# The root chain of the first attention stage, issued at the seventh matmul of the query product instead of ahead of it

## The chip, the cores and the metric

The kernel runs on one core of a Trainium2 chip. The metric is the device time of one execution in microseconds (us), the median of three runs. A profiled execution gives a trace of the five engines: PE (TensorE; its weight loads are listed apart as PEld), DVE (VectorE), ACT (ScalarE), POOL (GpSimd) and SP, which only issues DMAs here.

## What is computed

One layer of an encoder, for two sequences of 2048 tokens with 1024 features, all in float32. Two kinds of attention share one input projection:

```
h = rms_norm(x, norm_w)
q_a, k_a, v_a, g_a, q_b, k_b, v_b, g_b = split(h @ w_in)
q_a, k_a = rope(rms_norm(q_a)), rope(rms_norm(k_a))      # 8 query heads, 2 key heads of 64
o_a = window_attention(q_a, k_a, v_a, sink) * silu(g_a)   # +-128 tokens
o_b = neighbourhood_attention(q_b, k_b, v_b, rpb) * silu(g_b)
x = x + concat(o_a, o_b) @ w_out
y = x + (p @ w_ple) * sigmoid(x @ w_ple_gate)
```

The change lies in the first stage alone: branch a, the windowed attention.

## The kernel before

The kernel has three stages: windowed attention (token tiles f = 0 to 31, 16 of 128 tokens for each sequence), neighbourhood attention, and the output products. Each float32 operand of a product is split into a rounded part and a remainder, so that each product becomes three matmuls per block of 128 rows; splits are shared out between ACT (the rounded part) and VectorE or POOL (the remainder).

In the first stage, each token tile f passes `proj_a(f)` (L391), a generator with three products: `pk` (keys and values, 24 matmuls of 256 columns), `pq` (queries, 24 of 512) and `pg` (gate, 24 of 512). Attention of a tile is done by `unit_a(f, kv)` (L540), twice for each tile, once for each key head. Its steps are: `sc` (four heads of scores, each two matmuls and, in `softmax`, L214, one VectorE instruction that adds the mask and takes the row maximum, L217), then `exps` (L224: the negated maximum `nm`, L230; four exponentials on ACT, L232; the sink, L236 and L237; and after "den" the denominator L239, its reciprocal L240, a factor L241, and a gate product on POOL, L243), `pt` (three groups of four transposes of the weights, each split by L566 on ACT and L567 on VectorE), `po` (products with the values) and `fin` (two transposes `pgt` of the gate, then the output from L586 on ACT, two L589 and L590 on VectorE).

A list written out by hand, `PLAN_A` (L77), says at which share of a tile's projection cost each step of attention is issued. Projection matmuls of tile f + 2 fill TensorE between the steps of tile f. So in what this document calls a block, one token tile's worth of the stage, TensorE works first through `pq`, then `pg`, then `pk` of the next tile; the first half holds the unit of key head 0, the second that of key head 1. In the first half the four `sc` steps come after 2, 4, 4 and 5 matmuls of `pq`, the step "rest" (the second part of the split of the queries, `split_q`, L248: a copy on ACT, L252, a subtraction on VectorE, L254, a copy on POOL, L256) after 4 and 5, "den" after 11, "fin" after 14, and `pt` from 23.

TensorE's order is fixed by the source (`pinned`). On the other engines an instruction that isn't pinned takes the place in its engine's queue that a planner gives it when the kernel is built: among the instructions that it takes to be ready, the first in the source, so that others fill the gaps of a chain whose steps wait for each other. `P` (L155) pins an instruction behind whatever stands before it in the source on its engine. Each engine then works strictly in the order of its queue.

Around the change, on VectorE: when the last matmul of `pk` has been issued, `proj_a` emits the mean square (L398, L400, pinned), the sums of squares of the two key heads (L403), and then the **root chain**: L407 and L409 (the values under the roots), `rsqrt` (L123: two integer instructions L126 and L128, then three Newton rounds of L131, L132 and L133, on 128x3 values), the halving L411, the scaling of the keys L413, and the rotation `rope` (four POOL instructions, L426 to L429). The chain's results are used by `values` (L417, issued at the 16th matmul of `pq`, PV = 15), by the transposition of the keys in `keys_a` (L379, at the tenth matmul of `pg`) and by the tanh of the gate (L468). At the third and fifth matmul of `pq` the next token tile is split (`split`, L286: a pinned ACT cast L294, a POOL subtraction L295, and a load). At the tenth (PD = 9) `late` issues the gate of the tile before (L471, pinned).

PSUM is shared out by tags. `sc`, `pgt` and `pt` share three slots in turn: in each half, the third group of `pt` gets the slot that `pgt` had, and must wait until L590 has read `pgt`.

Of the kernel before, what the change touches and what calls it, by code (L numbers as in the profile page):

```python
# [11 lines left out]
F32 = mybir.dt.float32  # L12
# [3 lines left out]
ALU = mybir.AluOpType  # L16
# [6 lines left out]
HD = 64  # L23
NEG = -1.0e30
EPS = 1e-6
# [40 lines left out]
PG = (3, 6)  # L66
PV = 15
PD = 9
PB = (26, 30)
TAIL = 9300  # L70
HOLD = {"wa": 20, "wb": 12, "wp": 0}
# [18 lines left out]
def emit(ctx, tc, io):  # L90
    nc = tc.nc
# [31 lines left out]
    def rsqrt(pool, v, y, n, tag):  # L123
        i2 = pool.tile([128, n], I32, tag=tag + "i", name=tag + "i")
        a = pool.tile([128, n], F32, tag=tag + "a", name=tag + "a")
        nc.vector.tensor_scalar(out=i2, in0=v.bitcast(I32), scalar1=1, scalar2=None,  # L126
                                op0=ALU.logical_shift_right)
        nc.vector.tensor_scalar(out=y.bitcast(I32), in0=i2, scalar1=-1, scalar2=0x5F3759DF,  # L128
                                op0=ALU.mult, op1=ALU.add)
        for _ in range(3):  # L130
            nc.vector.scalar_tensor_tensor(out=a, in0=y, scalar=-0.5, in1=y, op0=ALU.mult, op1=ALU.mult)  # L131
            nc.vector.tensor_tensor(out=a, in0=a, in1=v, op=ALU.mult)  # L132
            nc.vector.scalar_tensor_tensor(out=y, in0=a, scalar=1.5, in1=y, op0=ALU.add, op1=ALU.mult)  # L133
# [21 lines left out]
    P = tc.keep_in_program_order  # L155
# [105 lines left out]
    ap = ab_stack.enter_context(tc.tile_pool(name="ab", bufs=1))  # L261
# [37 lines left out]
    def square(f, i):  # L299

        if f >= 2 * NT:
            return
        if i == 0:
            stats[f] = (ap.tile([128, 12], F32, tag="ssq", name="ssq", bufs=3),
                        ap.tile([128, 1], F32, tag="ee", name="ee", bufs=3))
        ssq, ee = stats[f]
        xn = staged.pop(("n", f, i))
        sqr = nc.scalar.activation(xn, xn, AF.Square, accum_out=ssq[:, 10 + i:11 + i])
        if f > 1:
            tc.keep_in_program_order(sqr)  # L310
            load_next()
        if i == 1:
            for dst, src in copies[:CP] if f >= 2 else ():
                tc.keep_in_program_order(nc.sync.dma_start(dst, src))
                copies.pop(0)
# [41 lines left out]
    for i in range(4):  # L357
        nc.vector.tensor_tensor(out=tab[i // 2][:, i % 2], in0=cs[:, i % 2],
                                in1=rw[:, i].unsqueeze(1).broadcast_to([128, NT, 16]), op=ALU.mult)
# [16 lines left out]
    last = {2 * NT - 2: 48, 4 * NT - 2: 24, 6 * NT - 2: 24}  # L376
    HX = {PB[0]: 0, PB[1]: 1}

# [12 lines left out]
    def proj_a(f):  # L391
        s, t = divmod(f, NT)
        xr, ms, (ssq, ee) = xt.pop(f), ms_a[:, f:f + 1], stats.pop(f)
        ka = 22 if f in last else KA
        early = 1 < f < 2 * NT - 1
        pk = ptile([128, 256], "pj", "pk")
        yield from project(pk, xr, lambda k, b: wx[:, k, b, :], 112)
        P(nc.vector.tensor_scalar(out=ms, in0=ssq[:, 10:11], scalar1=ssq[:, 11:12], scalar2=1.0 / DM,  # L398
                                  op0=ALU.add, op1=ALU.mult))
        P(nc.vector.tensor_scalar(out=ee, in0=ms, scalar1=EPS, scalar2=EPS * EPS, op0=ALU.mult, op1=ALU.add))  # L400
        sq2 = ap.tile([128, 512], F32, tag="sq", name="sq2", bufs=2)
        nc.scalar.activation(sq2[:, :128], pk[:, 0:128], AF.Square)
        nc.vector.tensor_reduce(out=ssq[:, 8:10], in_=sq2[:, :128].rearrange("p (h d) -> p h d", d=HD),  # L403
                                op=ALU.add, axis=AX.X)
        vr = ap.tile([128, 11], F32, tag="vr", name="vr", bufs=2)
        y = ap.tile([128, 12], F32, tag="y", name="y", bufs=4)
        nc.vector.tensor_scalar(out=vr[:, 8:10], in0=ssq[:, 8:10], scalar1=1.0 / HD, scalar2=ee,  # L407
                                op0=ALU.mult, op1=ALU.add)
        nc.vector.tensor_scalar(out=vr[:, 10:11], in0=ms, scalar1=EPS, scalar2=None, op0=ALU.add)  # L409
        rsqrt(ap, vr[:, 8:11], y[:, 8:11], 3, "rqk")  # L410
        nc.vector.tensor_scalar_mul(y[:, 11:12], y[:, 10:11], 0.5)  # L411
        kt = ap.tile([128, 4, HD], F32, tag="kt", name="kt", bufs=2)
        nc.vector.tensor_tensor(out=kt[:, 0:2, :], in0=pk[:, 0:128].rearrange("p (h d) -> p h d", d=HD),  # L413
                                in1=y[:, 8:10].unsqueeze(2).broadcast_to([128, 2, HD]), op=ALU.mult)
        pv = pk[:, 128:256].rearrange("p (h d) -> p h d", d=HD)

        def values():  # L417
            P(nc.scalar.activation(vv[:, t, :, 0, :], pv, AF.Copy, scale=y[:, 10:11]))
            P(nc.vector.scalar_tensor_tensor(out=vv[:, t, :, 1, :], in0=pv, scalar=y[:, 10:11],
                                             in1=vv[:, t, :, 0, :].bitcast(F32), op0=ALU.mult, op1=ALU.subtract))  # L420

        def rope(v, n, tb):
            r = ap.tile([128, 2, 8, 16], F32, tag="vr_", name="r", bufs=2)
            cb_ = tab[tb][:, 0, t, :].unsqueeze(1).broadcast_to([128, n, 16])
            sb_ = tab[tb][:, 1, t, :].unsqueeze(1).broadcast_to([128, n, 16])
            nc.gpsimd.tensor_tensor(out=r[:, 0, :n], in0=v[:, :, 0:16], in1=cb_, op=ALU.mult)  # L426
            nc.gpsimd.tensor_tensor(out=r[:, 1, :n, 0:8], in0=v[:, :, 8:16], in1=sb_[:, :, 0:8], op=ALU.mult)
            nc.gpsimd.tensor_tensor(out=r[:, 1, :n, 8:16], in0=v[:, :, 0:8], in1=sb_[:, :, 8:16], op=ALU.mult)
            nc.gpsimd.tensor_tensor(out=v[:, :, 0:16], in0=r[:, 0, :n], in1=r[:, 1, :n], op=ALU.add)  # L429
        rope(kt[:, 0:2, :], 2, 1)  # L430
        yield 0, False
        pq = ptile([128, 512], "pj", "pq")
        for i, c in enumerate(project(pq, xr, lambda k, b: w_q[k][:, b, :], 215)):
            if i in HS and early:
                split(f + 1, HS[i], P)
            if i - 4 in HN and f in last:
                square(f + 1, HN[i - 4])
            if i == PV:
                values()
            if i == PD and late:  # L440
                late.pop()()
            if i == PD + 1 and f == NT + 9:
                stats_b(0)
            yield c
            if i == ka:
                keys_a(kt, t)
        sq = ap.tile([128, 512], F32, tag="sq", name="sq", bufs=2)
        nc.scalar.activation(sq, pq, AF.Square)
        nc.vector.tensor_reduce(out=ssq[:, 0:8], in_=sq.rearrange("p (h d) -> p h d", d=HD), op=ALU.add, axis=AX.X)
        nc.vector.tensor_scalar(out=vr[:, 0:8], in0=ssq[:, 0:8], scalar1=1.0 / HD, scalar2=ee,  # L450
                                op0=ALU.mult, op1=ALU.add)
        rsqrt(ap, vr[:, 0:8], y[:, 0:8], 8, "rqa")
        q = ap.tile([128, 8, HD], F32, tag="qg", name="q", bufs=6)
        nc.vector.tensor_tensor(out=q, in0=pq.rearrange("p (h d) -> p h d", d=HD),  # L454
                                in1=y[:, 0:8].unsqueeze(2).broadcast_to([128, 8, HD]), op=ALU.mult)
        rope(q, 8, 0)
        yield 0, False
        pg = ptile([128, 512], "pj", "pg")
        for i, c in enumerate(project(pg, xr, lambda k, b: w_g[k][:, b, :], 215)):
            if i in HG and f > 0 and not early:  # L460
                split(f + 1, HG[i])
            if i in HN and f > 0 and f not in last:
                square(f + 1, HN[i])
            yield c
            if i + 24 == ka:
                keys_a(kt, t)
        gs = ap.tile([128, 512], F32, tag="qg", name="gs", bufs=6)
        nc.scalar.activation(gs, pg, AF.Tanh, scale=y[:, 11:12])  # L468

        def gate():  # L470
            P(nc.vector.scalar_tensor_tensor(out=gs, in0=gs, scalar=1.0, in1=pg, op0=ALU.add, op1=ALU.mult))  # L471
        if 0 < f < 2 * NT - 2:
            late.append(gate)
        else:
            gate()
        held[f] = q, gs, y
        if t == NT - 1:
            regroup(s)
        else:
            regroup_next()  # L480
        yield 0, False
# [129 lines left out]
    def proj_b(f):  # L611
# [10 lines left out]
        for i, c in enumerate(project(pk, xr, lambda k, b: ready("wa", k, w_qk)[:, b, :], 215)):  # L622
            at = i + 24 if f in last else i
            if i == PD and f == 2 * NT + 9:
                stats_b(1)
# [299 lines left out]
    with tc.tile_pool(name="c", bufs=1) as op:  # L925
# [192 lines left out]
        for m in range(7 * len(groups)):  # L1118
            n, i = divmod(m, 7)
# [104 lines left out]
```

## Time and profile before

| what | value |
|---|---|
| median of 3 runs | 2607.18 us (2605.81 to 2609.73) |
| profiled execution, its own time | 2603.58 us |
| its span, first to last instruction | 2601.7 us |
| TensorE busy in the span | 2547.1 us (98%) |
| VectorE busy | 1963.3 us (75%) |
| ScalarE busy | 1416.3 us (54%) |
| POOL busy | 789.2 us (30%) |
| granted TensorE clock, mean | 0.994 |

How to read the rows that follow: in a timeline or a chain of waits, the first number is the start in us from the span's start, the second the duration in us; then come the engine, the line of the kernel, the operation, the tiles (written <- read), the shapes, and after an x how many instructions the row holds. In brackets behind it stands the time that the engine was idle before, and what ended it. Rows of a wait list give the waiting engine, tile and line, then the one waited for, and the total in us, the number of times, and the longest wait.

### The profile page before, as it was taken

The page shows a single profiled execution, that of the slowest core. Times are in us where ns is not written, and L with a number is a line of the kernel's source. Part 1 is how long each engine was busy: PE and PEld are TensorE (multiplying, and loading weights), DVE is VectorE, ACT ScalarE, POOL GpSimd, SP SyncE. Part 2 cuts the span into 40 slices and gives each one's busy share as a digit, 9 for nine tenths or more (in the row PEclk, how much of TensorE's full clock was granted, in tenths as well). Part 3 has the DMA queues.
Part 4 walks back from the last instruction along what each step waited for, and adds up shares of the span by engine and source line. Part 5 has one row for each costly group of instructions (what it writes and reads, how often), then busy time and mean ns, then how long its engine had stood idle before and what let it go on. Part 6 is the DMA issues. An engine that isn't in the chain of part 4 may idle for free.

```text
span 2601.7 us, 47013 instructions
## 1 busy us (share of the span) xinstructions
PE 2547.1 (98%) x16080; PEld 2269.7 (87%) x16080; DVE 1963.3 (75%) x5702; ACT 1416.3 (54%) x3327; POOL 789.2 (30%) x996
## 2 busy tenths in 40 slices
PE   7999999999999999999999999999989999999999
PEld 6888888888877888888788888887989999999999
DVE  6888988889897788888888888888655648555454
ACT  5666666666675666666766666666432214222222
POOL 3333333333322333333233332321122423233321
PEclk9999999999999999999999999999999999999999
DMA  5333322111143564555654554457575445232221
GB/s 178 108 102 108 101 93 94 54 60 56 58 111 120 174 188 153 185 184 163 225 178 150 187 177 150 153 155 214 172 251 190 150 165 196 82 116 92 78 82 45
DMA packets 227519, 357.51 MB, mean 137 GB/s; under 512 B 37936, under 2 KB 115376, under 8 KB 222128
## 3 DMA queue, kind: packets, MB, share of 16 engines
q1 hardware_dynamic: 227280, 354.50, 42.8%
q8 instruction: 128, 2.10, 0.3%
q14 instruction: 111, 0.91, 0.1%
HBM read 266.33 MB, written 105.92 MB: 143 GB/s over the span
## 4 chain that ended last, share of the span: by engine, by line
PE 87%; DVE 5%; DMA 2%; ACT 2%; issue 2%; POOL 1%; SPq 0%; POOLq 0%; DVEq 0%; ACTq 0%
PE pqk L202 13%; PE pvg L202 12%; PE acca L1034 11%; PE accc L1034 9%; PE pg L202 6%; PE pq L202 5%; PE pob L202 4%; PE pple L202 3%; PE ptb L205 3%; PE scb L202 3%; PE pt L205 3%; PE po L202 3%; PE sc L202 3%; PE pk L202 3%; PE pout L202 3%
## 5 line engine op out<-in xcount | busy, mean ns | idle before, releaser
L232 ACT ACTIVATE s<-s,nm 128x384 f32<-128x384 f32 (+4 forms) x512 | 306.2, 599 | 340.6 <-DVE nm L228 185.0
L202 PE MATMUL pvg<-wb,xr 128*128 128x512 f32 x1536 | 455.2, 404 | 0.0
L202 PE MATMUL pqk<-wa,xr 128*128 128x512 f32 x1536 | 437.4, 407 | 0.0
L295 POOL TENSOR_TENSOR xr<-stx,xr 128x512 fp32r<-128x512 f32 x192 | 247.6, 1297 | 193.4 <-ACT xr L294 189.9
L202 PEld LDWEIGHTS pqk<-wa,xr 128*128 128x128 f32 x1536 | 267.5, 189 | 37.2
L202 PEld LDWEIGHTS pvg<-wb,xr 128*128 128x128 f32 x1536 | 267.4, 189 | 31.3
L202 PE MATMUL pg<-wb,xr 128*128 128x512 f32 x768 | 232.4, 410 | 4.1 <-DVE q L454 4.1
L202 PE MATMUL pq<-wa,xr 128*128 128x512 f32 x768 | 222.8, 404 | 3.6 <-ACT wa L147 2.8
L243 POOL TENSOR_TENSOR g<-qg,rd 128x256 f32<-128x256 f32 x64 | 39.7, 620 | 495.1 <-DVE rd L241 481.3
L1034 PE MATMUL acca<-opd,s 128*128 128x256 f32 x1344 | 164.6, 283 | 2.9 <-ACT r L1066 2.5
L1034 PEld LDWEIGHTS acca<-opd,s 128*128 128x128 f32 x1344 | 162.7, 192 | 3.6 <-ACT r L1066 2.7
L202 PEld LDWEIGHTS pq<-wa,xr 128*128 128x128 f32 x768 | 141.1, 191 | 28.3 <-ACT wa L147 3.4
L217 DVE CUSTOM_DVE_ANT_0 s<-scb,bias 128x288 f32<-128x288 f32 (+3 forms) x256 | 142.0, 555 | 29.1 <-PE scb L202 23.6
L202 PEld LDWEIGHTS pg<-wb,xr 128*128 128x128 f32 x768 | 137.9, 190 | 25.0 <-issue 4.6
L726 ACT CAST p_t<-ptb 96x384 fp32r<-96x384 f32 (+3 forms) x256 | 129.7, 508 | 54.1 <-PE ptb L205 52.3
L727 DVE TENSOR_TENSOR p_t<-ptb,p_t 96x384 fp32r<-96x384 f32 (+3 forms) x256 | 149.0, 584 | 9.1 <-ACT p_t L726 6.4
L607 ACT ACTIVATE ks_b<-pktb,wk 64x128 fp32r<-64x128 f32 x256 | 125.4, 490 | 49.1 <-DVE ks_b L608 40.6
L202 PEld LDWEIGHTS pob<-p_t,vw 128*128 128x128 f32 (+2 forms) x832 | 133.2, 190 | 20.8 <-DVE p_t L727 2.5
L608 DVE SCALAR_TENSOR_TENSOR ks_b<-pktb,wk,ks_b 64x128 fp32r<-64x128 f32 x256 | 115.1, 449 | 39.8 <-ACT ks_b L607 33.4
L202 PE MATMUL pob<-p_t,vw 128*128 128x256 f32 (+2 forms) x832 | 141.0, 283 | 2.0 <-DVE p_t L727 2.0
L1000 POOL TENSOR_TENSOR opd<-sum,opd 128x1024 fp32r<-128x1024 f32 x28 | 69.5, 2484 | 232.6 <-ACT opd L986 232.6
L217 DVE CUSTOM_DVE_ANT_0 s<-sc,mask 128x384 f32<-128x384 f32 (+1 forms) x256 | 135.8, 532 | 0.8
(197 smaller groups left out, 5909.1 us busy)
## 6 DMA issues: line engine op xcount, KB each, us to landing
stx<-x_b SPq DMA_DIRECT2D x128, 256.0 KB
vw<-v_d SPq DMA_DIRECT2D x112, 256.0 KB
stx<-x_a SPq DMA_DIRECT2D x64, 256.0 KB
stn<-x_n SPq DMA_DIRECT2D x64, 256.0 KB
v_d<-vb SPq DMA_DIRECT2D x64, 256.0 KB
x1r<-x_d SPq DMA_DIRECT2D x16, 1024.0 KB
y_t<-r SPq DMA_DIRECT2D x64, 256.0 KB
v_d<-vb SPq DMA_DIRECT2D x96, 128.0 KB
```

What stands on the lines that cost most here:

```text
L202: pinned(nc.tensor.matmul(out, lhsT, rhs, start=start, stop=stop))
L205: pinned(nc.tensor.transpose(out, in_, ident))
L217: nc.vector.tensor_tensor_reduce(out=s[:, :n], in0=ps[:, :n], in1=bias, scale=1.0, scalar=-3.0e38, op0=ALU.add, op1=ALU.max, accum_out=sm[ ...
L232: nc.scalar.activation(ss[i][:, :n], ss[i][:, :n], AF.Exp, bias=nm[:, i:i + 1], accum_out=den[:, i:i + 1])
L243: nc.gpsimd.tensor_tensor(out=g2, in0=gs.rearrange("p (h d) -> p h d", h=4), in1=rd.unsqueeze(2).broadcast_to([128, 4, HD]), op=ALU.mult)
L295: nc.gpsimd.tensor_tensor(out=lo, in0=raw, in1=hi.bitcast(F32), op=ALU.subtract)
L607: nc.scalar.activation(hi, pkt[a:a + 64, i], AF.Copy, scale=wk[a:a + 64, 1:2])
L608: nc.vector.scalar_tensor_tensor(out=lo, in0=pkt[a:a + 64, i], scalar=wk[a:a + 64, 1:2], in1=hi.bitcast(F32), op0=ALU.mult, op1=ALU.subtract)
L726: nc.scalar.copy(p_t[:kc, :nch, 0], pf)
L727: nc.vector.tensor_tensor(out=p_t[:kc, :nch, 1], in0=pf, in1=p_t[:kc, :nch, 0].bitcast(F32), op=ALU.subtract)
L1000: each(lambda x, y, z: eng.tensor_tensor(out=x, in0=y, in1=z, op=ALU.subtract), out, a, b)
L1034: pinned(nc.tensor.matmul(ps[:, kk], w[k][:, a, c:c + 128], o[:, b, k], start=i in (0, 1, 4) and kk == 0 and k == 0 and j == 0, stop=k == ...
```

## The change

The root chain, the scaling of the keys and their rotation become a function `roots`. For the first two token tiles it is called where the code stood; for all others at the seventh matmul of `pq` (PC = 6), which in the source is behind the four `sc` steps, `nm`, and the VectorE instruction of "rest" (L254). Its first instruction is pinned.

```diff
+PC = 6
...
-        nc.vector.tensor_scalar(out=vr[:, 8:10], in0=ssq[:, 8:10], scalar1=1.0 / HD, scalar2=ee,
-                                op0=ALU.mult, op1=ALU.add)
-        nc.vector.tensor_scalar(out=vr[:, 10:11], in0=ms, scalar1=EPS, scalar2=None, op0=ALU.add)
-        rsqrt(ap, vr[:, 8:11], y[:, 8:11], 3, "rqk")
-        nc.vector.tensor_scalar_mul(y[:, 11:12], y[:, 10:11], 0.5)
-        kt = ap.tile([128, 4, HD], F32, tag="kt", name="kt", bufs=2)
-        nc.vector.tensor_tensor(out=kt[:, 0:2, :], in0=pk[:, 0:128].rearrange("p (h d) -> p h d", d=HD),
-                                in1=y[:, 8:10].unsqueeze(2).broadcast_to([128, 2, HD]), op=ALU.mult)
...
-        rope(kt[:, 0:2, :], 2, 1)
+        kt = ap.tile([128, 4, HD], F32, tag="kt", name="kt", bufs=2)
+
+        def roots():
+
+            P(nc.vector.tensor_scalar(out=vr[:, 8:10], in0=ssq[:, 8:10], scalar1=1.0 / HD, scalar2=ee,
+                                      op0=ALU.mult, op1=ALU.add))
+            nc.vector.tensor_scalar(out=vr[:, 10:11], in0=ms, scalar1=EPS, scalar2=None, op0=ALU.add)
+            rsqrt(ap, vr[:, 8:11], y[:, 8:11], 3, "rqk")
+            nc.vector.tensor_scalar_mul(y[:, 11:12], y[:, 10:11], 0.5)
+            nc.vector.tensor_tensor(out=kt[:, 0:2, :], in0=pk[:, 0:128].rearrange("p (h d) -> p h d", d=HD),
+                                    in1=y[:, 8:10].unsqueeze(2).broadcast_to([128, 2, HD]), op=ALU.mult)
+            rope(kt[:, 0:2, :], 2, 1)
+        if f < 2:
+            roots()
         yield 0, False
         pq = ptile([128, 512], "pj", "pq")
         for i, c in enumerate(project(pq, xr, lambda k, b: w_q[k][:, b, :], 215)):
...
+            if i == PC and f > 1:
+                roots()
             if i == PV:
                 values()
```

## The prediction

> **What bounds the kernel now.** I read the page first, then the chain of waits over one block of the first attention stage, then the wait list of that stage, then the timeline of each engine in that block.
>
> ```profile
> PE 87%; DVE 5%; DMA 2%; ACT 2%; issue 2%; POOL 1%; SPq 0%; POOLq 0%; DVEq 0%; ACTq 0%
> ```
>
> TensorE is 87% of the chain that ended last. So an edit that moves only vector work counts only where it changes a wait of TensorE. The chain of one steady block (it starts with the query product at 309.95; start us, us, what) shows where such a wait is:
>
> ```profile
> 318.91 0.44 PE pt L205 x4
> ...
> 320.04 0.66 PE pt L205 x4
> ```
>
> Two groups of four transposes of the same size, 0.44 and 0.66 us: the third group (pt2) pays 0.66 - 0.44 = 0.22 us. The weight loads of TensorE in the timeline of the block, and the wait list from 60 to 770 us (us in total, times, longest), name the cause:
>
> ```profile
> 320.04 0.42 PEld L205 LDWEIGHTS pt<-ident,s 128*128 128x128 f32 x4 [0.44 <-DVE ot L590]
> ```
>
> ```profile
> PEld pt L205 <- DVE ot L590: 12.1, 26, 1.3
> ```
>
> pt2 needs the PSUM slot of pgt, and L590 is the last reader of pgt. It happens 26 times, nearly once in each block. **So the change is worth what it does to the end of L590 in the first half of a block**, 26 times over: 26 x 0.22 = 5.7 us if the wait goes altogether, and one for one in the other direction, since TensorE already waits there. VectorE in that half (start us, duration, instruction):
>
> ```profile
> 310.99 0.55 DVE L217 CUSTOM_DVE_ANT_0 s<-sc,mask 128x384 f32<-128x384 f32 x1
> ...
> 313.29 0.98 DVE L128 TENSOR_SCALAR y<-rqki 128x3 int32<-128x3 int32 x1
> 314.19 0.54 DVE L217 CUSTOM_DVE_ANT_0 s<-sc,mask 128x384 f32<-128x384 f32 x1
> ...
> 314.77 0.16 DVE L230 SCALAR_TENSOR_TENSOR nm<-mx,snk 128x4 f32<-128x4 f32 x1
> ...
> 315.05 0.15 DVE L133 SCALAR_TENSOR_TENSOR y<-rqka,y 128x3 f32<-128x3 f32 x1
> 315.24 0.69 DVE L254 TENSOR_TENSOR q<-pqt,q 64x512 fp32r<-64x512 f32 x1
> 315.96 0.16 DVE L131 SCALAR_TENSOR_TENSOR rqka<-y 128x3 f32<-128x3 f32 x1
> 316.16 0.69 DVE L471 SCALAR_TENSOR_TENSOR gs<-gs,pg 128x512 f32<-128x512 f32 x1
> 316.76 0.15 DVE L132 TENSOR_TENSOR rqka<-rqka,vr 128x3 f32<-128x3 f32 x1
> 316.95 0.16 DVE L133 SCALAR_TENSOR_TENSOR y<-rqka,y 128x3 f32<-128x3 f32 x1
> ...
> 317.74 0.15 DVE L411 TENSOR_SCALAR y<-y 128x1 f32<-128x1 f32 x1
> 317.81 0.28 DVE L413 TENSOR_TENSOR kt<-pk,y 128x128 f32<-128x128 f32 x1
> 318.00 0.15 DVE L239 TENSOR_TENSOR den<-den,es 128x4 f32<-128x4 f32 x1
> 318.26 0.18 DVE L240 RECIPROCAL rd<-den 128x4 f32<-128x4 f32 x1
> 318.47 0.23 DVE L241 TENSOR_SCALAR rd<-rd,y 128x4 f32<-128x4 f32 x1
> 318.61 0.85 DVE L589 TENSOR_TENSOR ot<-po,ot 64x256 f32<-64x256 f32 x2
> 319.56 0.42 DVE L590 TENSOR_TENSOR ot<-pgt,ot 128x256 f32<-128x256 f32 x1
> ```
>
> The root chain and the maxima alternate, so the last maximum starts at 314.19 only. The gate of the previous block (L471) falls into the chain too. L590 ends at 319.56 + 0.42 = 319.98.
>
> **The change, part by part.** Thirteen small VectorE instructions before the product (two sums, two integer steps, nine Newton steps), the halving L411, the product L413 and four POOL instructions of the rotation go to the seventh matmul. Nothing is added or taken away, and no DMA is issued by what moves. In the source it passes two splits of the next token tile (ACT casts, POOL subtractions, loads on SP), the maxima, nm, es, and L254. The first moved instruction is pinned behind the VectorE instruction ahead of it in the source, which is now L254. The gate L471 is pinned too, and what stands ahead of it is now L413 instead of L254. So the order becomes: four maxima, nm, es, L254, chain, L413, L471, and the denominator and L589, L590 where they fit.
>
> The maxima. The last score matmul and POOL's second subtraction:
>
> ```profile
> 311.98 0.51 PE L202 MATMUL sc<-ks_a,q 128*128 128x384 f32 x2
> ```
>
> ```profile
> 312.96 1.29 POOL L295 TENSOR_TENSOR xr<-stx,xr 128x512 fp32r<-128x512 f32 x1
> ```
>
> The last maximum can start at 311.98 + 0.51 = 312.49 and, as the fourth of 0.55 from 310.99, ends by 313.2, where it now ends at 314.73. But the next instruction is nm, which reads two tiles in SBUF, and POOL runs from 312.96 to 314.25. What nm does then is seen once, in the last block of the stage, where no chain stands between the maxima and nm (VectorE, then POOL):
>
> ```profile
> 753.60 1.22 DVE L230 SCALAR_TENSOR_TENSOR nm<-mx,snk 128x4 f32<-128x4 f32 x1
> 754.86 0.16 DVE L236 TENSOR_TENSOR es<-snk,nm 128x4 f32<-128x4 f32 x1
> ```
>
> ```profile
> 753.52 2.71 POOL L295 TENSOR_TENSOR xr<-stx,xr 128x512 fp32r<-128x512 f32 x2 [6.63 <-ACT xr L294]
> ```
>
> It took 1.22 us for 0.16. L128 above does the same: its 0.98 ends at 314.27, 0.02 behind POOL. So the hold that L128 pays today is paid by nm instead: nm ends at 314.27, where it now ends at 314.93, a gain of 0.66 and not 1.5. Behind nm on VectorE stand es, L254 and the whole chain; on ACT the four exponentials wait for it.
>
> The Trainium skill has this rule, and it speaks against the change: "SBUF — State Buffer", section "Who interferes with whom", says that a VectorE instruction with two SBUF inputs contends with a GpSimd instruction that reads SBUF, and that one with a single SBUF input outside the two-port modes does not. The trace agrees on both: nm took 1.22, the maxima 0.55. Without the rule the sum would be that of the first rival below.
>
> Then es at 314.27 + 0.04 (754.82 to 754.86) = 314.31, and L254 after it as after L133 now (315.20 to 315.24): 314.31 + 0.16 + 0.04 = 314.51. L254 holds its successor for 315.96 - 315.24 = 0.72: L407 at 315.23. It takes 0.23 like L241, its successor starts 0.04 later: L126 at 315.50. Now the chain runs almost alone, each step waiting for the one ahead: 316.95 to 317.74 is four steps, 0.197 each. From L126 to L411 are eleven steps, 2.17: L411 at 317.67, L413 (0.07 later, as now) at 317.74, L471 (0.19 later) at 317.93, its successor (0.60, as 316.16 to 316.76) at **318.53**. The keys are thus not late (L413 at 317.74, now 317.81). What is late next is what the gate now stands in front of: the denominator and the halves L589.
>
> How far those go into gaps of the chain is not shown for this order. A neighbouring block with shorter rows shows how they can:
>
> ```profile
> 413.30 0.15 DVE L239 TENSOR_TENSOR den<-den,es 128x4 f32<-128x4 f32 x1
> 413.42 0.15 DVE L411 TENSOR_SCALAR y<-y 128x1 f32<-128x1 f32 x1
> 413.49 0.28 DVE L413 TENSOR_TENSOR kt<-pk,y 128x128 f32<-128x128 f32 x1
> 413.69 0.17 DVE L240 RECIPROCAL rd<-den 128x4 f32<-128x4 f32 x1
> 413.77 0.39 DVE L589 TENSOR_TENSOR ot<-po,ot 64x256 f32<-64x256 f32 x1
> 414.08 0.22 DVE L241 TENSOR_SCALAR rd<-rd,y 128x4 f32<-128x4 f32 x1
> 414.34 0.43 DVE L589 TENSOR_TENSOR ot<-po,ot 64x256 f32<-64x256 f32 x1
> 414.87 0.42 DVE L590 TENSOR_TENSOR ot<-pgt,ot 128x256 f32<-128x256 f32 x1
> ```
>
> Here den goes in front of L411, and from L240 to the end of L590 it is 415.29 - 413.69 = 1.60. That is the value I take, because the chain now ends later after nm than before (L411 3.40 behind nm's end, now 2.81), so den and the first L589 are more likely to be ready in time: L590 ends at 318.53 + 1.60 = **320.13**, 0.15 later than now. The lower end is all three denominator steps in gaps (318.53 + 0.85 + 0.52 = 319.90, 0.08 earlier; 0.85 and 0.52 are L589 and from its end to that of L590 now). The upper end is none: from 318.00 to 319.98 is 1.98, so 320.51, 0.53 later.
>
> The sum: 26 x 0.15 = **+3.9 us**. The profiled execution (2603.58 us, 1.9 of it outside the span) would become 2607.5; the median of the runs shown, 2607.18, is 3.6 above it, and I forecast 2607.2 + 3.9 = **2611 us**. Hidden at no cost: the rotation on POOL, which has no work between L295 and it; and the second half, whose VectorE work starts behind L590 and shifts with TensorE.
>
> **The rivals.**
>
> *The wait at pt2 goes (faster).* If nm is not held, nm ends by 313.4 and all behind it comes 0.87 earlier: L590 at 320.13 - 0.87 = 319.26, 0.72 before now, more than the 0.44 that the weight load waits. TensorE gains 26 x 0.22 = 5.7 us: 2601.5. The same time comes out if L471 is placed behind L590 (0.60 earlier, also enough). For it: the last maximum really ends 1.5 earlier. Against it: the row of nm at 753.60, and the pin of L471. It decides from the point where L590 ends 0.44 earlier, before 319.54.
>
> *The gate pushes L590 out (slower by more).* The gaps of the chain stay empty, as in the block above, where L239 comes only behind L413, and L471 stands in front of everything. With den alone in a gap L240 starts at 318.53, and 319.98 - 318.26 = 1.72 brings L590 to 320.25, 0.27 later: 26 x 0.27 = 7.0, 2614. With none, 26 x 0.53 = 13.8: 2621. For it: in the steady block the planner found no gap that fitted. Against it: the chain is now longer behind nm.
>
> *Nothing comes of it.* The maxima come early, nm is held, two or three of the small steps fall in gaps, and L590 ends within 0.08 of today: 26 x 0.08 = 2 us, 2605 to 2609.
>
> **How the numbers follow.** A measurement of this kernel can tell about 0.2%, 5.2 us, from no change. Chances: the forecast (L590 0.08 to 0.22 later, 2609 to 2613) 0.42; pushed out further 0.30; nothing 0.14; the wait goes 0.14. The forecast lies within 0.2% for all but 0.10 of its part (its upper end, 26 x 0.22 = 5.7, is over the bound, and so is 0.20 with a few blocks more than the 26). So slower by over 0.2%: 0.30 + 0.10 = 0.40; within: 0.32 + 0.14 = 0.46; faster: 0.14 (5.7 us is just over 5.2; a partial gain is in the part before). Both signs have a share, so the range is wide: from 2601.5 of the first rival, to 2618, which leaves out only the emptier half of the second. The likeliest case's own range is 2609 to 2613.
>
> **What would show it.** In the first half of a block: four maxima in a row, the last ended by 313.3 in the frame above; nm of about 1 us, ending with POOL's second subtraction; L126 and L128 of 0.16 to 0.17 instead of 0.98; L471 directly behind L413; and L590 0.15 later against pt0 than now, with the pt2 group at about 0.8 us. The block, from one query product to the next, would be 0.15 longer. I am wrong if nm is short, if L471 is behind L590, or if the pt2 group is 0.44.

## The result, and the profile after

| kernel | median, range | runs |
|---|---|---|
| before | 2607.36 us (2605.38 to 2609.97) | 8 |
| after | 2614.27 us (2610.9 to 2617.83) | 8 |

The ratio is 1.0024 with a 95% interval of 1.0015 to 1.0033: the changed kernel is 6.9 us slower (3.9 to 8.6), a little over the bound of 0.2% that the prediction set. The forecast was 2611, with a range of 2601.5 to 2618. The two profiled executions lie further apart than the medians: that of after took 2617.83 us, 3.6 above its median, that of before 2603.58, 3.8 below. So the two traces are compared stretch by stretch, not by their spans.

On the page of after, the shares of the chain that ended last (87% PE and 5% DVE before) are now

```profile
PE 79%; DVE 13%; issue 2%; ACT 2%; DMA 2%; POOL 1%; SPq 0%; DVEq 0%; POOLq 0%; ACTq 0%
```

The chain now leaves TensorE for VectorE in the blocks of the first stage. A steady block of after, with its query product at 312.95, is 3.00 later in its trace than the block at 309.95 that the prediction reads, so 3.00 is to be taken off for a comparison. VectorE in its first half (start us, duration, instruction):

```profile
313.93 0.55 DVE L218 CUSTOM_DVE_ANT_0 s<-sc,mask 128x384 f32<-128x384 f32 x1
...
315.57 0.55 DVE L218 CUSTOM_DVE_ANT_0 s<-sc,mask 128x384 f32<-128x384 f32 x1
...
316.16 1.10 DVE L231 SCALAR_TENSOR_TENSOR nm<-mx,snk 128x4 f32<-128x4 f32 x1
...
318.46 0.17 DVE L127 TENSOR_SCALAR rqki<-vr 128x3 int32<-128x3 int32 x1
...
320.52 0.16 DVE L240 TENSOR_TENSOR den<-den,es 128x4 f32<-128x4 f32 x1
320.64 0.15 DVE L431 TENSOR_SCALAR y<-y 128x1 f32<-128x1 f32 x1
320.81 0.29 DVE L432 TENSOR_TENSOR kt<-pk,y 128x128 f32<-128x128 f32 x1
321.02 0.68 DVE L479 SCALAR_TENSOR_TENSOR gs<-gs,pg 128x512 f32<-128x512 f32 x1
321.61 0.17 DVE L241 RECIPROCAL rd<-den 128x4 f32<-128x4 f32 x1
...
322.79 0.42 DVE L598 TENSOR_TENSOR ot<-pgt,ot 128x256 f32<-128x256 f32 x1
```

Line numbers have moved: L205 is now L206, L217 L218, L230 L231, L240 L241, L254 L255, L407 L427, L411 L431, L413 L432, L471 L479, L567 L575, L590 L598. The four maxima stand in a row. `nm` takes 1.10 us and ends at 317.26; POOL's second subtraction, in POOL's timeline, ends at 315.95 + 1.29 = 317.24:

```profile
315.95 1.29 POOL L296 TENSOR_TENSOR xr<-stx,xr 128x512 fp32r<-128x512 f32 x1
```

The integer steps are short, the gate L479 stands directly behind L432, and L598 ends at 323.21, which is 320.21 in the frame of the prediction (319.98 before). The weight load of the third group of transposes and the group itself show what TensorE pays, and the wait list from 60 to 770 us (total, times, longest) that it pays it in nearly every block:

```profile
323.26 0.42 PEld L206 LDWEIGHTS pt<-ident,s 128*128 128x128 f32 x4 [0.66 <-DVE ot L598]
323.26 0.66 PE L206 MATMUL pt<-ident,s 128*128 128x128 f32 x4 [0.21 <-DVE ot L598]
```

```profile
PEld pt L206 <- DVE ot L598: 17.6, 25, 1.1
```

The load waits 0.66 us instead of 0.44, and TensorE now stands idle for 0.21 before a group that is as long as it was (0.66). The sign that the prediction gave, a group of about 0.8 us in the chain, can't be read there, because the chain now comes from L598; the idle time and the group together are 0.87. Over the 23 blocks of the two sequences that have no edge of a sequence in them, the median block took 23.64 us instead of 23.42.

### The profile page after: what moved, and what is told of

It is laid out like the page before. It is cut to its first block, busy times and chain, and to the rows that moved or that the text cites. A ratio compares the mean times of both kernels' runs of the same rounds, so it can differ in the third digit from the quotient of the medians.

```text
span 2616.1 us, 47008 instructions
## 1 busy us (share of the span) xinstructions
PE 2549.3 (97%) x16080; PEld 2272.2 (87%) x16080; DVE 1961.4 (75%) x5702; ACT 1417.2 (54%) x3327; POOL 790.9 (30%) x996
## 4 chain that ended last, share of the span: by engine, by line
PE 79%; DVE 13%; issue 2%; ACT 2%; DMA 2%; POOL 1%; SPq 0%; DVEq 0%; POOLq 0%; ACTq 0%
PE pqk L203 12%; PE pvg L203 12%; PE acca L1042 11%; PE accc L1042 9%; PE pg L203 5%; PE pob L203 3%; PE pple L203 3%; PE scb L203 3%; PE ptb L206 3%; PE pk L203 3%; PE pout L203 3%; PE sc L203 2%; PE pt L206 2%; DVE s L218 2%; PE pq L203 2%
## 5 line engine op out<-in xcount | busy, mean ns | idle before, releaser
L218 DVE CUSTOM_DVE_ANT_0 s<-scb,bias 128x288 f32<-128x288 f32 (+3 forms) x256 | 142.0, 556 | 28.8 <-PE scb L203 23.8
L218 DVE CUSTOM_DVE_ANT_0 s<-sc,mask 128x384 f32<-128x384 f32 (+1 forms) x256 | 132.4, 536 | 4.7 <-PE sc L203 1.5
```

Of the source, the lines that this page charges most:

```text
L218: nc.vector.tensor_tensor_reduce(out=s[:, :n], in0=ps[:, :n], in1=bias, scale=1.0, scalar=-3.0e38, op0=ALU.add, op1=ALU.max, accum_out=sm[ ...
```

## The experiments

Each was timed in five rounds beside the kernel before on the same chip; theory A in the expectations is the prediction's mechanism, that L598's end sets the block. The table collects what the traces show. The middle columns are medians over 23 steady blocks, in us from the first record of the query product (309.78 in the prediction's block; the starts of blocks given in the text are those of the chain of waits, 0.17 later). Where a kernel has the line numbers of before, the keys are L413 and the last reader is L590. "End" is the stretch from the end of the last steady block to the first matmul of the next stage.

| kernel | nm ends | keys start (L432) | last reader of pgt ends | block | end | ratio to before |
|---|---|---|---|---|---|---|
| before | 5.15 | 8.02 | 10.20 | 23.42 | 45.1 | |
| after | 4.48 | 8.02 | 10.42 | 23.64 | 50.5 | 1.0024 (1.0015 to 1.0033) |
| e2_gate_free | 4.47 | 8.02 | 9.82 | 23.07 | 49.9 | 0.9968 (0.9956 to 0.9980) |
| e3_copy_act | 3.69 | 7.23 | 9.63 | 23.05 | 49.8 | 0.9970 (0.9958 to 0.9981) |
| e4_both | 3.69 | 8.83 | 9.45 | 23.09 | 50.1 | 0.9978 (0.9969 to 0.9988) |
| e1_gate_first | 4.47 | 9.61 | 10.23 | 23.87 | 50.0 | 1.0043 (1.0030 to 1.0055) |
| e5_gate_first_values_late | 4.47 | 9.62 | 10.24 | 23.45 | 50.4 | 1.0015 (1.0006 to 1.0024) |
| e6_before_gate_free | 5.15 | 7.52 | 9.84 | 23.07 | 45.1 | 0.9971 (0.9960 to 0.9982) |
| e7_before_copy_act | 4.91 | 7.78 | 9.96 | 23.17 | 44.9 | 0.9979 (0.9970 to 0.9988) |
| e8_tile31_back | 4.47 | 8.02 | 10.42 | 23.62 | 44.6 | 1.0015 (1.0006 to 1.0024) |
| e9_gate_free_tile31_back | 4.48 | 8.02 | 9.83 | 23.07 | 46.2 | 0.9953 (0.9940 to 0.9967) |

**The gate, not pinned** (in the changed kernel):

```diff
-            P(nc.vector.scalar_tensor_tensor(out=gs, in0=gs, scalar=1.0, in1=pg, op0=ALU.add, op1=ALU.mult))
+            nc.vector.scalar_tensor_tensor(out=gs, in0=gs, scalar=1.0, in1=pg, op0=ALU.add, op1=ALU.mult)
```

> The changed kernel with the gate of the tile before not pinned; in VectorE's queue it then stands at the end of the second half of the block before, ahead of the last remainders of the weights. Theory A: 0.6 us less in front of the last reader of pgt, which ends at 319.6 in the frame of the prediction instead of 320.2; the wait of the third group of transposes goes nearly or wholly: steady block 23.2 to 23.25 us, total 2601 to 2604, faster than both kernels. Theory B: 23.64 and 2614. Theory C: no change, since the keys come at the same time, 2614.

2599.09 us against 2605.99. The planner puts the gate at the end of the second half of the block before. VectorE in the block whose query product starts at 305.97:

```profile
304.37 0.67 DVE L479 SCALAR_TENSOR_TENSOR gs<-gs,pg 128x512 f32<-128x512 f32 x1
...
309.20 1.07 DVE L231 SCALAR_TENSOR_TENSOR nm<-mx,snk 128x4 f32<-128x4 f32 x1
...
313.81 0.29 DVE L432 TENSOR_TENSOR kt<-pk,y 128x128 f32<-128x128 f32 x1
314.02 0.17 DVE L241 RECIPROCAL rd<-den 128x4 f32<-128x4 f32 x1
...
315.20 0.42 DVE L598 TENSOR_TENSOR ot<-pgt,ot 128x256 f32<-128x256 f32 x1
```

`nm` is as long as in after, and L432 at its place; L241 follows 0.21 behind L432 instead of 0.80, and L598 ends 0.60 earlier in the block, which is about what the gate held its successor in after (321.02 to 321.61). So the gate alone makes the difference between a loss and a gain, and the wait at the third group is gone. The block became shorter by 0.35 than before's, not by the 0.22 of that group. The chains of the two kernels show the rest. Before, behind the third group at 320.04:

```profile
322.66 0.78 PE sc L202 x4
...
332.14 0.51 PE pt L205 x4
```

With the gate free, the same three pieces (third group, scores, third group of the second half):

```profile
316.06 0.44 PE pt L206 x4
...
318.48 0.69 PE sc L203 x4
...
327.88 0.44 PE pt L206 x4
```

0.22 + 0.09 + 0.07 = 0.38, close to the 0.35: later steps of the block that were late along with the first wait are on time again.

**The hold of nm.** The copy on POOL that stands ahead of its second subtraction goes to ACT, so that POOL is done earlier:

```diff
-        nc.gpsimd.tensor_copy(q1[part][z:z + 64], q1[part][a:a + 64])
+        if part:
+            nc.scalar.copy(q1[part][z:z + 64], q1[part][a:a + 64])
+        else:
+            nc.gpsimd.tensor_copy(q1[part][z:z + 64], q1[part][a:a + 64])
```

> The changed kernel with one copy per block (the second part of the queries' first split, 64x512) on ACT instead of POOL, where it stands between the two subtractions of the next token tile; so POOL's second subtraction starts and ends 0.65 to 0.7 us earlier. Theory A and B alike: nm is held 0.7 us less and everything behind it comes 0.7 earlier, the last reader of pgt at 319.5 instead of 320.2: block 23.2 us, total 2601 to 2604. If nm's length does not hang on POOL: nm stays at 1.1 us and the total at 2614. Theory C: half of the 6.9 us back at most.

2599.88 us. POOL's two subtractions, and `nm`, in the block whose query product starts at 306.9:

```profile
307.83 2.55 POOL L299 TENSOR_TENSOR xr<-stx,xr 128x512 fp32r<-128x512 f32 x2 [3.03 <-ACT xr L298]
```

```profile
310.09 0.32 DVE L231 SCALAR_TENSOR_TENSOR nm<-mx,snk 128x4 f32<-128x4 f32 x1
```

POOL ends at 310.38 and `nm` at 310.41. In the median, nm, L432 and L598 all come 0.79 earlier: the hold passes through the whole chain without loss. The block stops at 23.05.

**Both**: the copy on ACT, and the gate issued ahead of the chain (`PD = 5` in place of 9).

> The copy on ACT and the gate ahead of the root chain together, on the changed kernel. If what counts is only when the last reader of pgt ends, and TensorE is the bound once it ends before 319.54 in the frame of the prediction, this gives no more than the better of the two: block 23.2 us, 2601 to 2604. If nm's hold and the gate cost TensorE in two different places, it gives the sum of both, 2598 or less.

2600.83 us. L598 ends 0.97 earlier than in after, but the block is 23.09. The gains don't add: once L598 ends by about 9.85, its end decides nothing.

**The gate ahead of the chain, alone:**

```diff
-PD = 9
+PD = 5
```

> The changed kernel with the gate of the tile before issued ahead of the root chain instead of behind it (PD = 5 instead of 9); nothing else. Theory A (the gate, pinned behind the scaled keys, stands in front of the denominator and the output of the unit before): the chain ends 0.6 us later, but the denominator and both output halves fill its gaps, so the last reader of pgt ends about 0.2 us earlier than in the changed kernel, as in the kernel before: steady block 23.42 us instead of 23.64, total about 2607 to 2609. Theory B (the place of the gate is nothing, the hold of nm behind POOL's subtraction is the whole cost): 23.64 and 2614 stay. Theory C (the keys and the values come too late): the chain ends later still, so slower than 2614.

2618.25 us against 2605.99: a miss for theory A; only theory C had it slower. L598 ended about where before's L590 does, 10.23, as expected, and the block still became longer, 23.87. The keys (L432) are now at 9.61. The wait list from 60 to 770 us shows who waits for them:

```profile
ACT vv L411 <- DVE kt L432: 62.2, 30, 2.8
...
PEld sc L203 <- DVE pr L575: 21.0, 53, 2.1
```

The first of these was 21.7 in after, where the second was 3.7. L411 is the copy of the values, pinned on ACT, which needs the token's root from the chain. ACT in one block:

```profile
323.11 0.37 ACT L411 ACTIVATE vv<-pk,y 128x128 fp32r<-128x128 f32 x1 [2.19 <-DVE kt L432]
323.38 0.58 ACT L574 CAST pr<-pt 128x512 fp32r<-128x512 f32 x1
```

While L411 waits 2.19 us, the rounded weights L574 stand behind it; so the remainders L575 are late, and they are the last readers of the `pt` slots that the next scores need. Whether that was it is tested by the next kernel.

**The same, with the values later** (`PV = 23` in place of 15, so that L411 no longer stands in front of L574):

> As e1 (changed kernel, gate ahead of the root chain), with the values of the tile issued at the 24th matmul of the query product instead of the 16th, so that on ACT they stand behind the first rounded part of the weights. In e1 the last reader of pgt ended at the same place of the block as in the kernel before (10.20 us behind the query product's start), and yet the block took 23.87 us. Theory D: the 0.45 us on top come from the values' copy on ACT, which waits for the late root chain and holds up the rounded weights behind it. Then the block is 23.42 us again, total 2606 to 2609. If the excess comes from the last reader of pgt after all, or from the keys: 23.8 and 2617.

2607.01 us against 2602.81; the block is 23.45, with L598 at 10.24 as in e1. So the 0.42 of e1's block came from L411's place on ACT. With that out of the way the block follows L598 again.

**Is the moved chain needed for the gain?** The kernel before, with the gate not pinned:

> The kernel before, with the gate not pinned: in VectorE's queue it moves from the middle of the root chain to the end of the block before. Theory A (all that counts is when the last reader of pgt ends): about 0.5 us less in front of it, 319.46 in the frame of the prediction, just inside the limit of 319.54; block 23.07 to 23.2 us, total 2598 to 2602, so the moved root chain is not needed for it. If the early maxima are what makes e2 fast: 23.42 and 2606.

2595.59 us against 2602.81; the block is 23.07, as in e2. It isn't needed. And the kernel before, with the copy on ACT:

> The kernel before with the copy on ACT instead of POOL, the same edit that made the changed kernel 14 us faster (e3). Theory A with the hold: here the integer steps of the chain pay for POOL, and what the second integer step no longer waits the first one does; the last maximum starts at about 314.1 instead of 314.2: block 23.42 us, total within 2 us of the kernel before. If the copy itself is what was dear (POOL's or VectorE's time, whatever waits): 23.07 and 2599 here too.

2597.34 us against 2602.81, where within 2 us of before was expected: a miss in size. VectorE (the third and fourth maximum lie around these):

```profile
309.71 0.86 DVE L126 TENSOR_SCALAR rqki<-vr 128x3 int32<-128x3 int32 x1
...
310.96 0.16 DVE L128 TENSOR_SCALAR y<-rqki 128x3 int32<-128x3 int32 x1
```

With POOL done earlier, L128 is no longer held (0.98 before), and L126 is held longer (0.28 before). On balance the chain is 0.24 earlier, and so is the end of L593 (L590 before); the block is 0.25 shorter. The same edit gave 0.79 at L598 in the changed kernel, where the hold falls on `nm` alone, and 0.24 here.

**The end of the stage.** The column "end" shows a second price that no step of the prediction has: in the traces, all the kernels so far with the moved chain took some 5 us more from the last steady block to the next stage. TensorE there, after:

```profile
755.67 0.61 PE L203 MATMUL sc<-ks_a,q 128*128 128x384 f32 x2 [1.74 <-DVE pr L575]
...
759.10 1.01 PE L203 MATMUL sc<-ks_a,q 128*128 128x384 f32 x2 [2.59 <-DVE mx L218]
759.90 1.05 PE L203 MATMUL po<-pr,vv 128*128 128x512 f32 x2
```

and before:

```profile
747.97 0.61 PE L202 MATMUL sc<-ks_a,q 128*128 128x384 f32 x2 [0.95 <-DVE mx L217]
...
749.32 0.59 PE L202 MATMUL sc<-ks_a,q 128*128 128x384 f32 x2 [0.51 <-DVE pr L567]
749.75 0.64 PE L202 MATMUL po<-pr,vv 128*128 128x512 f32 x2
```

The waits are 4.33 us instead of 1.46. VectorE in after tells why; L149 are the remainders of the next stage's weights, which fill VectorE there:

```profile
752.65 2.36 DVE L149 SCALAR_TENSOR_TENSOR wa<-wa,nw 128x512 fp32r<-128x512 f32 x2
754.93 0.68 DVE L575 TENSOR_TENSOR pr<-pt,pr 128x512 fp32r<-128x512 f32 x1
755.53 0.74 DVE L149 SCALAR_TENSOR_TENSOR wa<-wa,nw 128x512 fp32r<-128x512 f32 x1
756.29 0.71 DVE L389 SCALAR_TENSOR_TENSOR ks_a<-pkt,wk,ks_a 64x128 fp32r<-64x128 f32 x2
757.03 1.42 DVE L149 SCALAR_TENSOR_TENSOR wa<-wa,nw 128x512 fp32r<-128x512 f32 x2
758.48 0.56 DVE L218 CUSTOM_DVE_ANT_0 s<-sc,mask 128x384 f32<-128x384 f32 x1
```

Two of L149, then L575, and so on, and the first maximum only at 758.48; TensorE, which needs its slot, goes on at 759.10. In the queue of before that maximum stands ahead of the last L567:

```profile
747.36 0.55 DVE L217 CUSTOM_DVE_ANT_0 s<-sc,mask 128x384 f32<-128x384 f32 x1
...
748.50 0.68 DVE L567 TENSOR_TENSOR pr<-pt,pr 128x512 fp32r<-128x512 f32 x1
```

So the planner, given another source order, put the maximum behind other work. The test: the chain of token tile 31 alone stays where it stood.

```diff
-        if f < 2:
+        if f < 2 or f == 2 * NT - 1:
             roots()
...
-            if i == PC and f > 1:
+            if i == PC and 1 < f < 2 * NT - 1:
                 roots()
```

> The changed kernel, with the chain of token tile 31 alone issued where it stood before the change (tiles 2 to 30 stay at the seventh matmul). Theory F: the 5 us at the end of the stage (from the last steady block to the first matmul of the next stage 50.5 us against 45.1) come from one place in VectorE's queue. In the changed kernel the planner puts the first score maximum of the last half behind four more remainders of the next stage's weights, two of keys and one of the weights' transposes, so that the score slot is freed only at 759.4; with tile 31's chain in its old place the maximum stands ahead of them as before. Expected: that stretch 45.1 (44.8 to 45.6), steady blocks unchanged at 23.64, and 5.2 us less than the changed kernel in total: a ratio to the kernel before of 1.0004 (0.9993 to 1.0016). Rival G: the last blocks pay because every moved chain makes its block late and these are the blocks without a later tile to hide it: then one chain less gives back at most one block's 0.22, the stretch stays at 50 and the ratio at 1.0024.

2608.97 us against 2605.33. TensorE's waits are again those of before, and on VectorE the maximum is back ahead of L575, which follows at 752.76:

```profile
752.23 0.62 PE L203 MATMUL sc<-ks_a,q 128*128 128x384 f32 x2 [0.96 <-DVE mx L218]
...
753.59 0.59 PE L203 MATMUL sc<-ks_a,q 128*128 128x384 f32 x2 [0.50 <-DVE pr L575]
```

```profile
751.62 0.55 DVE L218 CUSTOM_DVE_ANT_0 s<-sc,mask 128x384 f32<-128x384 f32 x1
```

The stretch is 44.6, and the steady blocks have not changed (23.62). In the trace it gave back 6.0 us; in the times the ratio fell by 0.0009, or 2.3 us, where 5.2 was expected, and its interval (1.0006 to 1.0024) overlaps that of after. The two together, tile 31 back and the gate free:

> The changed kernel with the gate product not pinned and the chain of token tile 31 issued where it stood before the change. Theory F: the two edits touch different places, the steady blocks (23.07 in place of 23.64) and the end of the stage (45.1 in place of 49.9), and add up: 0.9968 less 4.8 of 2606 us, a ratio to the kernel before of 0.995 (0.994 to 0.996), under the kernel before with its gate free (0.9971). Rival G: the end stays at 49.9 and the ratio at 0.9968.

2594.39 us against 2605.33, the best of the changed kernels. The end is 46.2 instead of 49.9 in e2, and the ratio fell by 0.0015, or 3.9 us. Its interval (0.9940 to 0.9967) overlaps that of e6 (0.9960 to 0.9982), the kernel before with its gate free, so these two can't be ranked.

So the reordering is shown, and what it takes in a trace; what it costs in the times is not. e2 and e6 have the same steady block, 23.07, and ends of 49.9 and 45.1, and yet their ratios are 0.9968 and 0.9971.

## Why the prediction was right or wrong

- **What bounds the kernel: right.** Between 9.96 and 10.42, the block is the end of pgt's last reader plus 13.22 (e7 13.21, before 13.22, e5 13.21, after 13.22): one for one, as said. In that range e1 alone lies off the line, and e5 shows why; below about 9.85 the block stays at 23.05 to 23.09.
- **nm held: right.** Forecast 314.27 in its frame, measured 314.26. The Trainium skill's rule that a VectorE instruction with two SBUF inputs contends with a GpSimd instruction that reads SBUF ("SBUF — State Buffer", section "Who interferes with whom") agrees with the traces here: nm took 1.10 and ended 0.02 behind POOL, the maxima 0.55 beside it; in e3 nm took 0.32 and ended 0.03 behind POOL.
- **The chain alone: right to 0.03** up to the halving, L411 before and L431 after (317.67 forecast, 317.64 measured). The keys came 0.17 behind it instead of 0.07, with the denominator in front of the two; that is most of the 0.08 by which the gate's successor was late (318.53 forecast, 318.61 measured). From the reciprocal, L240 before, to the end of the last reader it took 1.60, as taken from the neighbouring block.
- **The sum of a block: right in kind, mis-sized.** L590 0.15 later was forecast, 0.22 measured in the median. Over 23 steady blocks this is 5.1 us; the forecast for 26 was 3.9. So the case that was forecast came, at the upper end of its 0.08 to 0.22. The second rival's 2614 is close to the measured time by coincidence: it had 1.72 behind the gate, and 1.60 was measured.
- **The price of the first rival: mis-sized.** "TensorE gains 26 x 0.22" looked at one group. The block had 0.35 to lose (e2, e3 and e6 stop at 23.05 to 23.07), because the scores and the second half's third group wait too in the wake of the first. The second of that rival's two mechanisms was right: with the gate (L479) out of the way, the kernel is faster than before, by 8.3 us (5.2 to 11.5 by the interval of e2), not 5.7.
- **The second half "shifts with TensorE", and no step for the end of the stage: the step that failed.** The prediction read one steady block and multiplied it. The last block has another queue, since the planner sorts all instructions that aren't pinned anew, and there a maximum moved behind other work, from ahead of the last L567 to the end of its row: +5.4 in the trace of after. In the times it is worth less: 2.3 us from after to e8, 3.9 from e2 to e9, and nothing that can be seen between e2 and e6; its size stays open.

The sum of the two, 10.5 us, is more than the 6.9 measured (up to 8.6 by the interval). In the profiled executions the blocks at the border between the sequences took about 1 us less in after, and the next stage 1.3 less (1038.5 against 1039.8); that brings it to 8.2, but the next stage's time also varies among the other kernels (1038.4 to 1041.5). The output products took 3.5 more in the trace of after (813.4 against 809.9; 807.8 to 812.3 in the others), and no experiment bears on that. One block waits for the load of a token tile (27.32 in after, 25.55 before, 24.85 to 27.83 in the others) and is left out of the comparison. What remains is not attributed. That the total lies in the range is thus in part luck: the range was as wide as the rivals made it, the likeliest case's own 2609 to 2613 was missed, and the end of the stage had no term.

## What to carry to other kernels

Taking work out of the way of an instruction gains only as far as the next thing that holds it: here nm ran into POOL, which the integer steps had met before, and the gate came to stand in front of what the gain was meant for. When a moved step pushes a pinned one, ask first whether that one can go elsewhere: with the gate free the block is 23.07, 0.35 us below before's, with the chain moved or not. And when a planner orders the queues, read the first and the last block of a stage apart from the steady one, since a changed source order may reorder them differently.

## What the runs showed of the hardware

The granted clock fell without a long gap. At the end of the stage in after, TensorE's gaps were 1.74 and 2.59 us with 0.85 us of matmuls between. The windows there (length, busy time and count of PE, PEld, DVE, ACT and POOL, granted clock, DMA share, GB/s):

```profile
757.00:760.00 3.00, 0.90 (x3) 0.90 (x4) 2.94 (x9) 0.00 (x0) 0.00 (x0) 0.53 0.47 156
760.00:765.00 5.00, 5.00 (x15) 3.94 (x14) 1.47 (x8) 3.29 (x10) 0.62 (x1) 0.60 0.14 32
```

The clock was 0.53 and then 0.60 over five busy microseconds, and the `po` pair took 1.05 us where before's took 0.64. From the last `sc` group to the next stage's first matmul it took 764.11 - 759.10 = 5.01 us instead of 752.04 - 749.32 = 2.72. So of the 5.4 us at the end, 2.9 are the longer waits and about 2.3 the lower clock. The Trainium skill ("TensorE: Matmul & The Clock Gate", Part 1) gives a window of about 3.4 us without work as what halves the clock; here neither gap alone was that long.

The trace of e9 shows the same behind shorter gaps, of 1.16 and 0.51 us: from 740 to 743 us the granted clock was 0.50, and from the last `sc` group to the next stage's first matmul it took 743.20 - 738.90 = 4.30 us, where e8 took 756.30 - 753.59 = 2.71 behind gaps of 0.96 and 0.50. That is the 1.6 us by which e9's end is longer than e8's 44.6.
